# An output projection by seven products of quarters in place of eight, with sums of weight quarters made earlier in the kernel

## The chip, the cores and the metric

The kernel runs on one core of a Trainium2 chip. The metric is the device time of one execution in microseconds (us), the median of 3 runs. Five engines work side by side, each through its own list of instructions in a fixed order: TensorE (PE, matmuls; its weight loads are called PEld), VectorE (DVE), ScalarE (ACT), GpSimd (POOL) and SyncE (SP), which here issues the DMA transfers. A wait holds back all that stands behind it in the same list.

## The reference

One layer on x of 1024 frames by 1024 features, all in float32:

```
h = rmsnorm(x) * norm_w
parts = h @ w_in + b_in             # 5656 columns, cut into 16 segments
y = concat(hgrn2(parts), gla(parts), mlstm(parts))     # 4 heads of 128 from each, 1536 columns
x = x + y @ w_out                   # 1024x1536 by 1536x1024
return rmsnorm(x) * final_norm_w
```

The three mixers are chunked linear attentions with gates: trees of small DVE operations, small matmuls and states. The change touches only the product `y @ w_out`, what feeds it, and the places between the input projections where new work is put.

## The kernel before, in words

**Splitting.** [...] So each operand is kept as a high part (ACT copies and rounds it) and a low part (DVE subtracts the high part from the original), and each product is three matmuls into one PSUM tile: high by high, high by low, low by high. `load_w` (L214 to L228) does it for a weight block of 128x1024: one DMA of 512 KB into `wraw` (two buffers in turn, L222), ACT makes `whi` (L223), DVE makes `wlo` (L224); `whi` and `wlo` have three buffers each. The normalised input lies in sixteen tiles `hT`, `HI[k]` and `LO[k]`.

**Projections.** `projections` (a generator) walks the segments: for the HGRN2 heads h = 0 to 3 the projections f, q, v, z, then q, k, v, z of GLA, then those of the mLSTM, the last one called mz3. `proj_nt` loads a block and runs 24 matmuls of 512 columns for each half, and DVE moves each half out of PSUM (L350). `Weave` puts the small matmuls of the mixers between them by costs written in the generators, and the order of PE is kept as it is written (`manual_schedule`). The order on DVE, ACT and SP is set by the scheduler, and is fixed when the kernel runs. The finished heads go out to DRAM (`ydram`), and the last two, in `ys`, stay on the chip.

**Output projection (L973 to L1073), outside the manual order.** Twelve blocks of `wout` (128x1024) are split, nine of them into the slots of `hT` and others as they come free (L991 to L997). `load_y` brings 128 frames of y back and splits them (L1007 to L1012). There are 8 frame tiles, 2 halves of the columns and 12 blocks k; `out_matmuls` (L1020 to L1022) has the three matmuls of each, so 8 x 2 x 12 x 3 = 576 matmuls of 512 columns. The very last half is done in two parts of 256 columns, so that the page counts 540 of 512 and 72 of 256. `out_part` adds x (L1027), sums squares (ACT, L1029) and multiplies by the norm's weight (L1031); `out_store` finishes the norm and writes (L1036 to L1043).

Of the kernel before, what the change touches and what calls it, by code (L numbers as in the profile page):

```python
# [7 lines left out]
F32 = mybir.dt.float32  # L8
# [6 lines left out]
T = 1024  # L15
# [116 lines left out]
def kernel(ctx: ExitStack, tc: tile.TileContext, x, xt, wt, wide, cols, vbias, wa2, wout, fw, masks, sel,  # L132
# [58 lines left out]
    bq = const.tile([128, 2], F32, name="bq")  # L191

# [38 lines left out]
    HI = [ht.tile([128, T], F32R, name="hT") for _ in range(KC)]  # L231
    LO = [ht.tile([128, T], F32R, name="hT") for _ in range(KC)]
# [168 lines left out]
    def proj_z(name):  # L401
        z, piece = z_piece(name)
        yield from proj_nt(*piece)
        return z
# [400 lines left out]
    def ml_chain(w, r, ready, PQK, Vs, ogs, gates, ys, zs, done):  # L805
# [83 lines left out]
    outs, als, gated, last = [], [], [], []  # L889
    LAST = []  # L890
# [16 lines left out]
    def projections():  # L907
# [54 lines left out]
        LAST.extend(ys)  # L962
# [5 lines left out]

    with tc.manual_schedule(engines={mybir.EngineType.PE}):
        w.run(projections())  # L970
    ys = LAST


    fwb = fp.tile([128, D], F32, name="al", bufs=2)
    nc.sync.dma_start(fwb, bass.AP(tensor=fw.tensor, offset=fw.offset, ap=[[0, 128], [1, D]]))
    WO, raws = [], []
    for k in range(12):
        if k < 3:
            WO.append(load_w(wout[k * 128:(k + 1) * 128, :]))
            continue  # L980
        if k in (3, 5):
            raws = big.tile([128, 2, 1024], F32, name="big")
            raws = [raws[:, 0], raws[:, 1]]
        elif k in (7, 8):
            raws = [wp.tile([128, 1024], F32, name="wraw", bufs=2)]
        elif k == 9:
            raws = [att[:, j].rearrange("p c t -> p (c t)") for j in range(2)]
        elif k == 11:
            raws = [wk.tile([128, 1024], F32, name="S", bufs=1)]
        raw = raws.pop(0)  # L990
        nc.sync.dma_start(raw, wout[k * 128:(k + 1) * 128, :])  # L991
        if k < 11:
            hi, lo = ht.tile([128, 1024], F32R, name="hT"), ht.tile([128, 1024], F32R, name="hT")
        else:
            hi, lo = fp.tile([128, 1024], F32R, name="al", bufs=2), fp.tile([128, 1024], F32R, name="f")
        nc.scalar.activation(hi, raw, AF.Copy)
        nc.vector.tensor_sub(lo, raw, hi.bitcast(F32))  # L997
        WO.append((hi, lo))
    def load_y(i):
        ts = slice(i * 128, (i + 1) * 128)  # L1000
        yh = big.tile([128, 12, 128], F32R, name="big")
        yl = big.tile([128, 12, 128], F32R, name="big")
        yb = big.tile([128, 2, 640], F32, name="big") if i < 2 else None
        for a in (0, 5):
            yr = yb[:, a // 5] if i < 2 else wp.tile([128, 1024], F32, name="wraw", bufs=2)[:, 0:640]
            yr = yr.rearrange("p (k t) -> p k t", k=5)
            nc.sync.dma_start(yr, ydram[a:a + 5, :, ts].rearrange("k p t -> p k t"))  # L1007
            nc.scalar.activation(yh[:, a:a + 5], yr, AF.Copy)
            nc.vector.tensor_sub(yl[:, a:a + 5], yr, yh[:, a:a + 5].bitcast(F32))
        for h in range(2):  # L1010
            nc.scalar.activation(yh[:, 10 + h], ys[h][:, ts], AF.Copy)
            nc.vector.tensor_sub(yl[:, 10 + h], ys[h][:, ts], yh[:, 10 + h].bitcast(F32))  # L1012
        xr = wk.tile([128, D], F32, name="zg")
        nc.sync.dma_start(xr, x[ts, :])
        st = wk.tile([128, 8], F32, name="st", bufs=4)
        return yh, yl, xr, st, (wk.tile([128, 512], F32, name="kd"), wk.tile([128, 512], F32, name="osb"))

    def out_matmuls(p, y, ns, k):
        hi, lo = WO[k]
        nc.tensor.matmul(p, y[0][:, k], hi[:, ns], start=k == 0, stop=False)  # L1020
        nc.tensor.matmul(p, y[0][:, k], lo[:, ns], start=False, stop=False)  # L1021
        nc.tensor.matmul(p, y[1][:, k], hi[:, ns], start=False, stop=k == 11)  # L1022

    def out_part(p, y, ns, part):

        xr, st, xo = y[2:]
        nc.vector.tensor_add(xr[:, ns], p, xr[:, ns])  # L1027
        sq = wk.tile([128, 768], F32, name="qm")
        nc.scalar.activation(sq[:, 0:ns.stop - ns.start], xr[:, ns], AF.Square, accum_out=st[:, part:part + 1])  # L1029
        h = ns.start // 512  # L1030
        nc.vector.tensor_mul(xo[h][:, ns.start - 512 * h:ns.stop - 512 * h], xr[:, ns], fwb[:, ns])  # L1031

    def out_store(i, y, parts):
        st, xo = y[3:]
        if parts == 3:
            nc.gpsimd.tensor_add(st[:, 0:1], st[:, 0:1], st[:, 1:2])  # L1036
        nc.vector.tensor_scalar(st[:, 4:5], st[:, 0:1], 1.0 / D, EPS, op0=OP.mult, op1=OP.add)
        nc.vector.scalar_tensor_tensor(st[:, 5:6], st[:, parts - 1:parts], 1.0 / D, st[:, 4:5], op0=OP.mult, op1=OP.add)
        nc.gpsimd.tensor_tensor(st[:, 6:7], st[:, 5:6], mhalf[:, 0:1], op=OP.pow)
        nc.scalar.activation(xo[0], xo[0], AF.Copy, scale=st[:, 6:7])  # L1040
        nc.vector.tensor_scalar(xo[1], xo[1], st[:, 6:7], None, op0=OP.mult)
        for h in (1, 0):
            nc.sync.dma_start(out[i * 128:(i + 1) * 128, 512 * h:512 * h + 512], xo[h])  # L1043

    halves = [slice(0, 512), slice(512, D)]
    tiles = [load_y(0), load_y(1)]
    ps = [[pl.tile([128, 512], F32, name=nm) for _ in range(2)] for pl, nm in ((pmain, "pm"), (po, "po"))]
    for k in range(12):
        for y, pp in zip(tiles, ps):
            for half in range(2):  # L1050
                out_matmuls(pp[half], y, halves[half], k)
    for i in range(NC):
        y = tiles[i] if i < 2 else load_y(i)
        parts = halves if i < NC - 1 else [halves[0], slice(512, 768), slice(768, D)]
        for a, ns in enumerate(parts):
            if i < 2:
                p = ps[i][a]
            else:
                p = pmain.tile([128, 512], F32, name="pm")[:, 0:ns.stop - ns.start]
                for k in range(12):  # L1060
                    out_matmuls(p, y, ns, k)
            out_part(p, y, ns, a)
        out_store(i, y, len(parts))


def _layout(inputs):
# [78 lines left out]
```

## Time and profile before

| | us |
|---|---|
| median of 3 runs (lowest, highest) | 777.31 (776.87, 777.75) |
| profiled execution: its own time | 775.69 |
| its span in the trace | 773.9 |
| PE busy in the span | 764.1 (99%) |
| DVE, ACT, POOL busy | 411.8, 331.6, 67.1 |
| start of the first matmul of the output projection | 634.01 |
| start of the last matmul | 767.14 |

The span is the time from the first to the last instruction in the trace; 1.8 us of the profiled execution lie outside it. The profiled execution is 1.6 us below the median. Matmuls overlap, so that the time one costs is the distance from its start to the next start, not its length.

### The profile page before, as it was taken

What the parts mean: (1) busy time and instruction counts of PE and PEld (TensorE: products, weight loads), DVE (VectorE), ACT (ScalarE), POOL (GpSimd) and SP (SyncE); (2) the same over time, 40 slices, a digit from 0 to 9 for tenths busy, and PEclk for the clock granted to TensorE, in tenths of its full rate; (3) what the DMA queues carried; (4) which work ended last, traced back from release to release, by engine and by line L of the source; (5) the groups of instructions that cost most, each with busy time, mean ns of one, the idle gap of its engine ahead of it and who ended that gap; (6) DMA issues with size and microseconds to landing.
All of it is one profiled execution on the core that took longest, in us unless ns stands there. A gap on an engine that the chain in (4) does not pass through costs nothing.

```text
span 773.9 us, 14500 instructions
## 1 busy us (share of the span) xinstructions
PE 764.1 (99%) x5991; PEld 660.9 (85%) x5991; DVE 411.8 (53%) x923; ACT 331.6 (43%) x747; POOL 67.1 (9%) x107
## 2 busy tenths in 40 slices
PE   9999999999999999999999999999999999999996
PEld 6889887898887898889988899988899988888886
DVE  7886577584467257325732755343754473532332
ACT  7553689532625404271324532552614592332211
POOL 2001210010200100040001300110000000100000
PEclk9999999999999999999999999999999999999999
DMA  8410120012021102112010202032204342252211
GB/s 284 133 55 26 58 87 28 30 56 62 28 83 33 52 30 63 55 39 72 23 68 28 82 28 63 9 83 87 74 8 165 108 151 89 94 172 90 89 54 55
DMA packets 29810, 55.96 MB, mean 72 GB/s; under 512 B 2656, under 2 KB 16480, under 8 KB 29744
## 3 DMA queue, kind: packets, MB, share of 16 engines
q1 hardware_dynamic: 29072, 54.51, 21.6%
q8 instruction: 47, 0.77, 0.4%
q0 software_dynamic: 672, 0.53, 0.3%
q14 instruction: 19, 0.16, 0.1%
HBM read 45.39 MB, written 9.63 MB: 71 GB/s over the span
## 4 chain that ended last, share of the span: by engine, by line
PE 89%; ACT 4%; DVE 2%; issue 2%; DMA 1%; SPq 1%; POOL 0%; POOLq 0%; DVEq 0%; ACTq 0%
PE pm L338 11%; PE pm L340 11%; PE pm L339 11%; PE pm L370 9%; PE pm L371 8%; PE pm L372 8%; PE pm L1022 5%; PE pm L1020 5%; PE pm L1021 5%; PE po L573 2%; PE po L575 2%; PE pt L558 1%; PE pt L488 1%; PE tp L532 1%; PE pt L457 1%
## 5 line engine op out<-in xcount | busy, mean ns | idle before, releaser
L338 PE MATMUL pm<-hT,whi 128*128 128x512 f32 x400 | 162.5, 406 | 0.0
L340 PE MATMUL pm<-hT,wlo 128*128 128x512 f32 x400 | 156.3, 391 | 0.0
L339 PE MATMUL pm<-hT,whi 128*128 128x512 f32 x400 | 156.2, 391 | 0.0
L370 PE MATMUL pm<-whi,hT 128*128 128x256 f32 (+1 forms) x488 | 142.7, 292 | 0.0
L371 PE MATMUL pm<-wlo,hT 128*128 128x256 f32 (+1 forms) x488 | 138.4, 284 | 0.0
L372 PE MATMUL pm<-whi,hT 128*128 128x256 f32 (+1 forms) x488 | 138.3, 283 | 0.0
L223 ACT ACTIVATE whi<-wraw 128x1024 fp32r<-128x1024 f32 (+4 forms) x50 | 48.7, 977 | 113.1 <-PE pm L372 57.0
L370 PEld LDWEIGHTS pm<-whi,hT 128*128 128x128 f32 x488 | 93.1, 191 | 3.1 <-issue 2.2
L371 PEld LDWEIGHTS pm<-wlo,hT 128*128 128x128 f32 x488 | 93.3, 191 | 0.3
L372 PEld LDWEIGHTS pm<-whi,hT 128*128 128x128 f32 x488 | 93.2, 191 | 0.0
L340 PEld LDWEIGHTS pm<-hT,wlo 128*128 128x128 f32 x400 | 75.1, 188 | 16.6
L338 PEld LDWEIGHTS pm<-hT,whi 128*128 128x128 f32 x400 | 75.2, 188 | 16.0 <-issue 1.5
L339 PEld LDWEIGHTS pm<-hT,whi 128*128 128x128 f32 x400 | 75.3, 188 | 13.5
L224 DVE TENSOR_TENSOR wlo<-wraw,whi 128x1024 fp32r<-128x1024 f32 (+4 forms) x50 | 55.9, 1122 | 18.5 <-ACT whi L223 18.5
L377 DVE SCALAR_TENSOR_TENSOR big<-pm,rs,vb 128x256 f32<-128x256 f32 x72 | 32.0, 454 | 51.0 <-PE pm L372 50.7
L1020 PE MATMUL pm<-hT,big 128*128 128x512 f32 (+1 forms) x120 | 45.4, 378 | 0.0
L1022 PE MATMUL pm<-hT,big 128*128 128x512 f32 (+1 forms) x120 | 45.4, 378 | 0.0
L1021 PE MATMUL pm<-hT,big 128*128 128x512 f32 (+1 forms) x120 | 45.2, 376 | 0.0
L499 ACT ACTIVATE att<-dc 32x128 f32<-32x128 f32 (+1 forms) x48 | 16.5, 344 | 48.6 <-DVE dc L479 48.1
L1027 DVE TENSOR_TENSOR zg<-pm,zg 128x512 f32<-128x512 f32 (+1 forms) x15 | 9.8, 653 | 50.6 <-PE pm L1022 33.8
L350 DVE TENSOR_TENSOR f<-pm,RSB 128x512 f32<-128x512 f32 x18 | 12.4, 687 | 39.0 <-PE pm L340 38.9
L350 DVE TENSOR_TENSOR zg<-pm,RSB 128x512 f32<-128x512 f32 x22 | 15.2, 690 | 31.0 <-PE pm L340 30.9
(303 smaller groups left out, 1317.4 us busy)
## 6 DMA issues: line engine op xcount, KB each, us to landing
wraw<-in_wt_dram SPq DMA_DIRECT2D x39, 512.0 KB, 3.5
zg<-in_x_dram SPq DMA_DIRECT2D x8, 512.0 KB, 3.9
wraw<-ydram SPq DMA_DIRECT2D x12, 320.0 KB, 3.6
big<-in_xt_dram SPq DMA_DIRECT2D x5, 512.0 KB, 4.9
wraw<-in_wout_dram SPq DMA_DIRECT2D x5, 512.0 KB, 4.3
ydram<-zg SPq DMA_DIRECT2D x8, 256.5 KB, 2.1
big<-in_wout_dram SPq DMA_DIRECT2D x4, 512.0 KB, 6.9
out_dram<-kd SPq DMA_DIRECT2D x8, 256.0 KB, 2.4
```

The lines of the kernel that those rows point to most:

```text
L223: nc.scalar.activation(hi[:, s], raw[:, s], AF.Copy)
L224: nc.vector.tensor_sub(lo[:, s], raw[:, s], hi[:, s].bitcast(F32))
L338: nc.tensor.matmul(p, hi[:, ks], HI[k][:, s], start=k == 0, stop=False)
L339: nc.tensor.matmul(p, hi[:, ks], LO[k][:, s], start=False, stop=False)
L340: nc.tensor.matmul(p, lo[:, ks], HI[k][:, s], start=False, stop=k == KC - 1)
L370: nc.tensor.matmul(p, HI[k][:, ts], hi[:, ks], start=k == 0, stop=False)
L371: nc.tensor.matmul(p, HI[k][:, ts], lo[:, ks], start=False, stop=False)
L372: nc.tensor.matmul(p, LO[k][:, ts], hi[:, ks], start=False, stop=k == KC - 1)
L377: nc.vector.scalar_tensor_tensor(dst, p, rs[:, c:c + 1], b, op0=OP.mult, op1=OP.add)
L1020: nc.tensor.matmul(p, y[0][:, k], hi[:, ns], start=k == 0, stop=False)
L1021: nc.tensor.matmul(p, y[0][:, k], lo[:, ns], start=False, stop=False)
L1022: nc.tensor.matmul(p, y[1][:, k], hi[:, ns], start=False, stop=k == 11)
```

## The change

The output projection is cut into quarters: frames in two halves, the 1536 columns of y in two halves of 768, the columns of the result in two halves of 512. A11, A12, A21, A22 are the quarters of y (first figure frames), and `wq[0]` to `wq[3]` those of the weights, which the host now lays out as [4, 3, 128, 1024]. Seven products of quarters, in the order 1, 2, 6, 7, 5, 4, 3, take the place of eight. Each has 4 tiles of 128 frames, 6 blocks of 128 in the depth, and 3 matmuls of 512 columns; the last tile of the last product is again done in two parts of 256. Forms of y (sums and differences of quarters) are made in place by DVE: `s2` (L1050 to L1052, 18 subtractions of 128x512) and `s1` (L1057, 6). `a_form` splits a form (ACT L1040, DVE L1041, six each of 128x512), `b_form` loads and splits three blocks of weights (L1027 to L1029). Products that share an output are added in PSUM where they follow each other (1 and 2, 6 and 7), otherwise by DVE.

Four of the weight forms are sums of quarters. `sum_steps` makes them in 12 steps between the projections: each loads two blocks of 512 KB into the two `wraw` buffers, adds them (DVE, L979), and writes 512 KB to `wsum` in DRAM. The order of PE in the output projection is now fixed as written. PE's order before it is the same as it was.

```
+    wsum = tc.dram_tile([4, 3, 128, 1024], F32, name="wsum")
+    def sum_steps():
+        for dst, a, b in ((0, wq[0], wq[1]), (2, wq[1], wq[3]), (1, wsum[0], wq[3]), (3, wsum[1], wq[2])):
+            for i in range(3):
+                ra, rb = (wp.tile([128, 1024], F32, name="wraw", bufs=2) for _ in range(2))
+                nc.sync.dma_start(ra, a[i])
+                nc.sync.dma_start(rb, b[i])
+                nc.vector.tensor_add(ra, ra, rb)
+                nc.sync.dma_start(wsum[dst, i], ra)
+                yield
+    sums = sum_steps()
...
                 for pce in pieces:
                     yield from proj_nt(*pce)
+                    next(sums, None)
...
                 zs.append((yield from proj_z(f"z{h}")))
+                next(sums, None)
...
             Q, K = yield from gla_qk(r)
+            next(sums, None)
...
                 zs.append((yield from proj_z(f"gz{2 * r + a}")))
+                next(sums, None)
...
-    HI = [ht.tile([128, T], F32R, name="hT") for _ in range(KC)]
-    LO = [ht.tile([128, T], F32R, name="hT") for _ in range(KC)]
+    HI, LO = zip(*[[ht.tile([128, T], F32R, name="hT") for _ in range(2)] for _ in range(KC)])
...
+                dst = y_tile(4 + h)[:, 1] if r else ys[h]
+                nc.vector.tensor_mul(dst[:, s], ys[h][:, s], zs[h][:, 1 + 512 * half:513 + 512 * half])
...
+        hts = [ht.tile([128, 1024], F32R, name="hT") for _ in range(16)]
+        w0 = [wp.tile([128, 1024], F32R, name=nm, bufs=3) for _ in range(3) for nm in ("whi", "wlo")]
+        ASET = [hts[0:6], hts[6:12]]
+        BSET = [w0, hts[12:16] + al2]
...
+        def s2(i):
+            t = wk.tile([128, 768], F32, name="qm")[:, 0:512]
+            nc.vector.tensor_sub(A11(i), A21(i), A11(i))
+            nc.vector.tensor_sub(t, A22(i), A11(i))
+            nc.vector.tensor_sub(A12(i), A12(i), t)
+            return t
...
+        def product(c, p, a, b, first, last, cols=slice(0, 512)):
+            for i in range(6):
...
+                nc.tensor.matmul(p[:, cols], ahi, bhi, start=first and i == 0, stop=False, skip_group_check=True)
+                nc.tensor.matmul(p[:, cols], ahi, blo, start=False, stop=False, skip_group_check=True)
+                nc.tensor.matmul(p[:, cols], alo, bhi, start=False, stop=last and i == 5, skip_group_check=True)
...
+        a1, b1 = a_form(A11), b_form(wq[0])
...
+        for c in range(4):
+            product(c, pa[c], a1, b1, True, False)
+            nc.scalar.activation(P1[:, c], pa[c], AF.Copy)
+        a2, b2 = a_form(A12), b_form(wq[2])
+        for c in range(4):
+            product(c, pa[c], a2, b2, False, True)
+        a6, b6 = a_form(s2), b_form(wsum[1])
...
```

In SP's list, from one load of projection weights early in the kernel on, these are the transfers of the kernel before (`wt` are weights of a projection, `vb` is a bias):

```order
L222 DMA wraw<-in_wt_dram 128x1024 x3
L357 DMA vb<-in_vbias_dram 128x256
L222 DMA wraw<-in_wt_dram 128x1024 x3
L517 DMA ydram<-zg 128x511
L514 DMA ydram<-zg 128x513
```

and these those of the changed one from the same load on, with the numbers of the buffers (`wq` are quarters of the output weights):

```order
L224 DMA wraw_904<-in_wt_dram 128x1024
L977 DMA wraw_1108<-in_wq_dram 128x1024
L978 DMA wraw_1109<-in_wq_dram 128x1024
L980 DMA wsum_479<-wraw_1108 128x1024
L224 DMA wraw_1114<-in_wt_dram 128x1024
L977 DMA wraw_1193<-in_wq_dram 128x1024
L358 DMA vb_1735<-in_vbias_dram 128x256
L978 DMA wraw_1194<-in_wq_dram 128x1024
L980 DMA wsum_479<-wraw_1193 128x1024
L224 DMA wraw_1200<-in_wt_dram 128x1024
```

Between any two of these weights now stand two loads and a write, and of the two buffers in turn the first holds L977's block until it is written, the second takes L978's block and then the next weight.

On DVE, where the tree of head 1 begins, before (L350 is the last half of q, L433 and L438 the tree, L695 and L696 a GLA gate):

```order
L437 TENSOR_TENSOR f<-f 128x128
L350 TENSOR_TENSOR zg<-pm,RSB 128x512
L695 TENSOR_SCALAR po<-po,pc 128x512 x2
L696 TENSOR_TENSOR al<-po,al 128x512
L433 COPY_PREDICATED dc<-mk_88,pt 128x32x3
L438 TENSOR_TENSOR big<-big,f 128x128x3
```

and after (each line number one higher):

```order
L351 TENSOR_TENSOR zg<-pm,RSB 128x512
L979 TENSOR_TENSOR wraw<-wraw 128x1024
L696 TENSOR_SCALAR po<-po,pc 128x512 x2
L434 COPY_PREDICATED dc<-mk_88,pt 128x32x3
L439 TENSOR_TENSOR big<-big,f 128x128x3
```

The sum of one step (L979, the fifth of the twelve) now stands ahead of the tree.

On DVE at the passage to the output projection the kernel before has this (the two L350 are the first and the last half of mz3, L997 the low parts of `wout` blocks, L1009 and L1012 those of y):

```order
L350 TENSOR_TENSOR zg<-pm,RSB 128x512
L997 TENSOR_TENSOR hT<-big,hT 128x1024
L833 TENSOR_TENSOR f<-f,zg 128x512
L997 TENSOR_TENSOR hT<-big,hT 128x1024
L1012 TENSOR_TENSOR big<-f,big 128x128
L997 TENSOR_TENSOR hT<-big,hT 128x1024
L350 TENSOR_TENSOR zg<-pm,RSB 128x512
L997 TENSOR_TENSOR hT<-big,hT 128x1024
L1009 TENSOR_TENSOR big<-big 128x640 x2
```

The changed one has, behind the first half of mz3, two L1041, an L1050, an L835 and an L1050, and then this (L1041 are low parts of A11 and then of A12, the L351 is the last half of mz3, and the L1029 is the low part of the third weight block of product 1):

```order
L1051 TENSOR_TENSOR qm<-big 128x512
L1057 TENSOR_TENSOR big<-big 128x512
L1041 TENSOR_TENSOR hT<-big,hT 128x512 x2
L1051 TENSOR_TENSOR qm<-big 128x512
L1057 TENSOR_TENSOR big<-big 128x512
L1041 TENSOR_TENSOR hT<-big,hT 128x512
L1041 TENSOR_TENSOR hT<-att,hT 128x512
L1041 TENSOR_TENSOR hT<-big,hT 128x512
L351 TENSOR_TENSOR zg<-pm,RSB 128x512
L1041 TENSOR_TENSOR hT<-big,hT 128x512
L1050 TENSOR_TENSOR big<-big 128x512 x2
L1029 TENSOR_TENSOR wlo<-wraw,whi 128x1024
```

From the first L1041 to the L1029 that is 18 operations of 128x512: eight L1041, eight of `s1` and `s2`, one L835 and one L351.

## Rows read from the trace of the kernel before

**Rows 1.** Which engines are busy, over the whole span (page).

```profile
PE 764.1 (99%) x5991; PEld 660.9 (85%) x5991; DVE 411.8 (53%) x923; ACT 331.6 (43%) x747; POOL 67.1 (9%) x107
```

**Rows 2.** By stretch: us, busy us by engine, PE's granted clock, DMA share, GB/s.

```profile
614.80:624.00 9.20, 9.20 (x48) 7.70 (x47) 4.47 (x12) 7.73 (x25) 2.42 (x4) 1.00 0.76 242
...
634.00:767.50 133.50, 133.42 (x613) 109.66 (x611) 48.12 (x92) 34.22 (x74) 6.34 (x9) 1.00 0.28 89
```

**Rows 3.** The same for L1020 alone, one of the three matmul lines.

```profile
634.00:768.00 134.00, 77.30 (x204) 38.16 (x203) 1.00 0.27 89
```

**Rows 4.** PE in order of time: start, length, then what ran; the output projection's first matmul.

```profile
634.01 0.39 PE L1020 MATMUL pm<-whi,big 128*128 128x512 f32 x1
```

**Rows 5.** PE in order of time, matmuls of 256 columns.

```profile
760.38 0.28 PE L1020 MATMUL pm<-hT,big 128*128 128x256 f32 x1
760.49 0.28 PE L1021 MATMUL pm<-hT,big 128*128 128x256 f32 x1
```

**Rows 6.** In order of time, the end: last matmul, last store's issue.

```profile
767.14 0.28 PE L1022 MATMUL pm<-al,big 128*128 128x256 f32 x1
770.27 0.38 SPq L1043 DMA_DIRECT2D out_dram<-kd  x1
```

**Rows 7.** In order of time, DVE and PE around the passage.

```profile
627.76 0.69 DVE L833 TENSOR_TENSOR f<-f,zg 128x512 f32<-128x512 f32 x1
628.37 0.68 DVE L350 TENSOR_TENSOR zg<-pm,RSB 128x512 f32<-128x512 f32 x1
629.67 0.40 PE L340 MATMUL pm<-hT,wlo 128*128 128x512 f32 x1
634.44 0.68 DVE L350 TENSOR_TENSOR zg<-pm,RSB 128x512 f32<-128x512 f32 x1
```

**Rows 8.** Groups of DVE from 600 us: busy us, mean ns, idle before.

```profile
L1031 DVE TENSOR_TENSOR kd<-zg,al 128x512 f32<-128x512 f32 x8 | 5.5, 689 | 0.9 <-DMA out_dram<-kd 0.7
```

**Rows 9.** In order of time, splitting of weights: ACT, DVE, SP's next load.

```profile
47.24 1.23 DVE L224 TENSOR_TENSOR wlo<-wraw,whi 128x1024 fp32r<-128x1024 f32 x1 [0.42 <-ACT whi L223]
48.49 0.33 SPq L222 DMA_DIRECT2D wraw<-in_wt_dram  x1
73.31 2.39 DVE L224 TENSOR_TENSOR wlo<-wraw,whi 128x1024 fp32r<-128x1024 f32 x2
92.30 1.06 ACT L223 ACTIVATE whi<-wraw 128x1024 fp32r<-128x1024 f32 x1
104.28 1.06 ACT L223 ACTIVATE whi<-wraw 128x1024 fp32r<-128x1024 f32 x1 [2.80 <-PE pm L339]
```

**Rows 10.** DMA issues (page): KB each, median us to landing.

```profile
wraw<-in_wt_dram SPq DMA_DIRECT2D x39, 512.0 KB, 3.5
ydram<-zg SPq DMA_DIRECT2D x8, 256.5 KB, 2.1
```

**Rows 11.** In order of time, tree of head 1: DVE's first and PE's wait.

```profile
110.46 0.69 DVE L350 TENSOR_TENSOR zg<-pm,RSB 128x512 f32<-128x512 f32 x1 [1.65 <-PE pm L340]
111.39 1.42 DVE L695 TENSOR_SCALAR po<-po,pc 128x512 f32<-128x512 f32 x2 [0.23 <-PE po L682]
122.75 0.45 PE L457 MATMUL pt<-big 128*32 128x16 f32 x32 [0.39 <-DVE dc L433]
```

**Rows 12.** By stretch, as 2, behind the last matmul.

```profile
767.50:771.50 4.00, 0.00 (x0) 0.00 (x0) 1.45 (x4) 1.23 (x3) 0.54 (x1) 1.00 0.20 77
771.50:772.00 0.50, 0.00 (x0) 0.00 (x0) 0.00 (x0) 0.00 (x0) 0.00 (x0) 0.68 1.01 389
```

**Rows 13.** PE in order of time, the kernel's first matmuls.

```profile
7.70 0.63 PE L296 MATMUL pm<-hT,whi 128*128 128x512 f32 x1
8.12 0.63 PE L297 MATMUL pm<-hT,whi 128*128 128x512 f32 x1
10.61 0.40 PE L297 MATMUL po<-hT,whi 128*128 128x512 f32 x1
10.84 0.39 PE L298 MATMUL po<-hT,wlo 128*128 128x512 f32 x1
```

More of the change, by code (lines that the diff above doesn't have):

```diff
@@ L131, with kernel @@
 @with_exitstack
-def kernel(ctx: ExitStack, tc: tile.TileContext, x, xt, wt, wide, cols, vbias, wa2, wout, fw, masks, sel,
+def kernel(ctx: ExitStack, tc: tile.TileContext, x, xt, wt, wide, cols, vbias, wa2, wq, fw, masks, sel,
                       ident_in, out):
@@ L191 @@
     bq = const.tile([128, 2], F32, name="bq")
+    fwb = const.tile([128, D], F32, name="fwb")
+    P1 = const.tile([128, 4, 512], F32, name="P1")
     def lower_bound():
@@ L967, in gla_tail, with y_tile @@
                         lambda: len(outs) >= 8 + 4 * r and len(vs) > 0, outs)
+    Y = {}
+    def y_tile(i):
+        if i not in Y:
+            Y[i] = att.rearrange("p h c t -> p h (c t)") if i == 5 else \
+                big.tile([128, 2, 1040], F32, name="big")[:, :, 0:T]
+        return Y[i]
     with tc.manual_schedule(engines={mybir.EngineType.PE}):
         w.run(projections())
[L971 to L975 removed]
@@ L976 @@
[L976 to L1031, printed above, removed]
@@ L1045 @@
[L1045 to L1063, printed above, removed]
+        nc.sync.dma_start(fwb, bass.AP(tensor=fw.tensor, offset=fw.offset, ap=[[0, 128], [1, D]]))
@@ new lines @@
+        for i in (0, 1, 2, 3):
+            y_tile(i)
+        for kh in range(2):
+            for i in range(6):
+                if kh * 6 + i < 10:
+                    for th in range(2):
+                        s = slice(512 * th, 512 * th + 512)
+                        nc.sync.dma_start(Y[i][:, kh, s], ydram[6 * kh + i, :, s])
+        hts = [ht.tile([128, 1024], F32R, name="hT") for _ in range(16)]
+        w0 = [wp.tile([128, 1024], F32R, name=nm, bufs=3) for _ in range(3) for nm in ("whi", "wlo")]
@@ new lines, with b_form @@
+        al2 = [fp.tile([128, 1024], F32R, name="al", bufs=2) for _ in range(2)]
+        ASET = [hts[0:6], hts[6:12]]
+        BSET = [w0, hts[12:16] + al2]
+        made = [0, 0]
+        def b_form(src):
+            t = BSET[made[1] % 2]
+            made[1] += 1
+            for i in range(3):
+                raw = wp.tile([128, 1024], F32, name="wraw", bufs=2)
+                nc.sync.dma_start(raw, src[i])
+                nc.scalar.activation(t[2 * i], raw, AF.Copy)
+                nc.vector.tensor_sub(t[2 * i + 1], raw, t[2 * i].bitcast(F32))
+            return t
@@ new lines, in a_form @@
+        def a_form(src):
+            t = ASET[made[0] % 2]
+            made[0] += 1
+            for i in range(6):
+                s = slice(512 * (i % 2), 512 * (i % 2) + 512)
+                raw = src(i)
+                hi, lo = t[i // 2 * 2][:, s], t[i // 2 * 2 + 1][:, s]
+                nc.scalar.activation(hi, raw, AF.Copy)
+                nc.vector.tensor_sub(lo, raw, hi.bitcast(F32))
+            return t
+        quarter = lambda th, kh: lambda i: Y[i][:, kh, 512 * th:512 * th + 512]
@@ new lines, with load_x @@
+        stats = const.tile([128, NC, 8], F32, name="stats")
+        U2 = [wk.tile([128, 512], F32, name=nm) for nm in ("osb", "osb", "kd", "kd")]
+        xt_of = [fp.tile([128, T], F32, name="f") for _ in range(3)] + [wk.tile([128, 1 + T], F32, name="zg")[:, 0:T] for _ in range(2)] \
+            + [wk.tile([128, 1024], F32, name="S", bufs=1), RSB]
+        xt_of = [[t[:, 0:512], t[:, 512:1024]] for t in xt_of]
+        junk = dc.rearrange("p h c x -> p (h c x)")
+        def load_x(cs):
+            for c in cs:
+                if c == 7:
+                    xt_of.append([wk.tile([128, 768], F32, name="qm")[:, 0:512] for _ in range(2)])
+                for h in range(2):
+                    nc.sync.dma_start(xt_of[c][h], x[128 * c:128 * c + 128, 512 * h:512 * h + 512])
@@ new lines, in xs, with rows_done, store @@
+        def xs(c, cols):
+            h = cols.start // 512
+            return xt_of[c][h][:, cols.start - 512 * h:cols.stop - 512 * h]
+        def rows_done(c, cols, part):
+            xr = xs(c, cols)
+            nc.scalar.activation(junk[:, 0:cols.stop - cols.start], xr, AF.Square, accum_out=stats[:, c, part:part + 1])
+            nc.vector.tensor_mul(xr, xr, fwb[:, cols])
+        def store(c, parts):
+            st, xr = stats[:, c], xt_of[c]
+            if parts == 3:
+                nc.gpsimd.tensor_add(st[:, 0:1], st[:, 0:1], st[:, 1:2])
+            nc.vector.tensor_scalar(st[:, 4:5], st[:, 0:1], 1.0 / D, EPS, op0=OP.mult, op1=OP.add)
+            nc.vector.scalar_tensor_tensor(st[:, 5:6], st[:, parts - 1:parts], 1.0 / D, st[:, 4:5], op0=OP.mult, op1=OP.add)
+            nc.gpsimd.tensor_tensor(st[:, 6:7], st[:, 5:6], mhalf[:, 0:1], op=OP.pow)
+            nc.scalar.activation(xr[0], xr[0], AF.Copy, scale=st[:, 6:7])
+            nc.vector.tensor_scalar(xr[1], xr[1], st[:, 6:7], None, op0=OP.mult)
+            for h in (1, 0):
+                nc.sync.dma_start(out[c * 128:(c + 1) * 128, 512 * h:512 * h + 512], xr[h])
@@ new lines @@
+        L, R = slice(0, 512), slice(512, D)
+        banks = lambda tags: [pl.tile([128, 512], F32, name=nm) for pl, nm in tags for _ in range(2)]
+        tags_a, tags_b = ((pmain, "pm"), (po, "po")), ((ptree, "pt"), (ptr, "tp"))
+        a1, b1 = a_form(A11), b_form(wq[0])
+        pa = banks(tags_a)
+        load_x(range(4))
+        for c in range(4):
+            product(c, pa[c], a1, b1, True, False)
+            nc.scalar.activation(P1[:, c], pa[c], AF.Copy)
+        a2, b2 = a_form(A12), b_form(wq[2])
@@ new lines @@
+        for c in range(4):
+            product(c, pa[c], a2, b2, False, True)
+        a6, b6 = a_form(s2), b_form(wsum[1])
+        pb = banks(tags_b)
+        for c in range(4):
+            nc.vector.tensor_add(xs(c, L), pa[c], xs(c, L))
+            rows_done(c, L, 0)
+        for c in range(4):
+            product(c, pb[c], a6, b6, True, False)
+            nc.vector.tensor_sub(U2[c], P1[:, c], pb[c])
+        a7, b7 = a_form(A11), b_form(wsum[2])
+        load_x(range(4, NC))
+        for c in range(4):
+            product(c, pb[c], a7, b7, False, True)
+            nc.vector.tensor_sub(P1[:, c], P1[:, c], pb[c])
+            nc.vector.tensor_sub(xs(c, R), xs(c, R), U2[c])
@@ new lines @@
+        a5, b5 = a_form(s1), b_form(wsum[0])
+        pa = banks(tags_a)
+        for c in range(4):
+            product(c, pa[c], a5, b5, True, False)
+            nc.vector.tensor_sub(xs(c + 4, R), xs(c + 4, R), P1[:, c])
+            nc.vector.tensor_add(xs(c + 4, R), pa[c], xs(c + 4, R))
+            rows_done(c + 4, R, 1)
+        a4, b4 = a_form(A22), b_form(wsum[3])
+        pb = banks(tags_b)
+        for c in range(4):
+            product(c, pb[c], a4, b4, True, True)
+            nc.vector.tensor_add(xs(c + 4, L), P1[:, c], xs(c + 4, L))
+            nc.vector.tensor_add(xs(c + 4, L), pb[c], xs(c + 4, L))
+            rows_done(c + 4, L, 0)
+            store(c + 4, 2)
@@ L1066, in _layout @@
+        a3, b3 = a_form(A12), b_form(wq[3])
+        for c in range(4):
+            parts = [R] if c < 3 else [slice(512, 768), slice(768, D)]
+            for n, cols in enumerate(parts):
+                pc_ = slice(cols.start - 512, cols.stop - 512)
+                product(c, pa[c], a3, b3, False, True, pc_)
+                nc.vector.tensor_add(xs(c, cols), pa[c][:, pc_], xs(c, cols))
+                rows_done(c, cols, 1 + n)
+            store(c, 1 + len(parts))
 def _layout(inputs):
```

30 lines of the change are left out of this document (13 added, 17 removed).

## The prediction

> **What bounds the kernel now.** I read the busy times first: PE works for 764.1 of 773.9 us, every other engine for half of that or less [rows 1]. Then the stretch that the change rewrites: from the first matmul of the output projection to the last PE has no gap worth naming (133.42 us busy in 133.5), while DVE works 48.12 us and the DMA engines 0.28 of the time [rows 2]. So time falls away only where matmuls do, and any wait that is put on PE is paid in full, unless it falls behind the last matmul. The row for one of the three matmul lines counts 204 [rows 3], so 612 in all: 540 of 512 columns and 72 of 256. The first starts at 634.01 [rows 4], the last at 767.14 and, with 0.28 us, ends at 767.42 [rows 6]: 133.4 us. Matmuls of 256 columns start 0.11 us apart [rows 5]. That leaves (133.4 - 72 x 0.11) / 540 = 0.232 us for one of 512. Behind the last matmul come 6.5 us of norm and store, which the change keeps in form: the last piece is again of 256 columns, and the store is again two transfers (the second is issued at 770.27 before [rows 6]).
>
> **Term 1, matmuls removed.** 7 x 4 x 6 x 3 = 504 in place of 576. By form it is 486 of 512 columns and 36 of 256: 486 x 0.2324 + 36 x 0.11 = 116.9 us. That is 16.5 less. The other bound is an eighth of the whole, 133.4 / 8 = 16.7. Nothing hides beside it, because PE was busy throughout.
>
> **Term 2, the passage to product 1.** Before, PE goes on from the last projection without a gap (busy before and after 634 [rows 2]), since three blocks of `wout` had been split in advance. Product 1 needs three blocks too, but `whi` and `wlo` have three buffers, and one of them holds the weights of mz3 until its last matmul. So the third block can be split only behind 634.2. What decides is DVE's list, which is fixed. Its subtraction for that third block (L1029) stands behind 18 operations of 128x512 that begin with the first low part of A11. That first one needs HI[0], whose last reader starts at 629.67 and takes 0.40 us [rows 7]; ACT's copy needs 0.6 us more, so DVE begins at about 630.8. Operations of 512 columns follow each other at 0.61 us when DVE has work queued (627.76 to 628.37 [rows 7]); alone one takes 0.689 [rows 8]. 18 of them last 11.0 to 12.4 us, then the subtraction itself 1.23 [rows 9]: the low part is there at 643.0 to 644.4. One among the 18 is the eviction of mz3's last half, which could run at 634.44 before [rows 7], earlier than its turn comes here, so it adds no wait. PE, which starts product 1 at 634.01, wants this block at its 14th matmul (first tile, fifth block of depth): 634.0 + 13 x 0.232 = 637.0. PE waits 6.0 to 7.4 us. I take +6.5. Lower bound 3, if DVE can start on the forms earlier than I read; upper bound 9, if the loads of y come late, since two `s1` operations ahead of that subtraction read the last pieces: 20 transfers of 256 KB are 5.2 MB, and at 242 GB/s [rows 2] that takes 21 us. If they start where that stretch does, at 614.8, and come in the order in which they are issued, the two thirds that those 18 operations read are there at 629, all at 636; I take no delay.
>
> **Term 3, the clock.** [...] What half speed costs is seen at the kernel's beginning: matmuls start 0.42 us apart (7.70, 8.12) until about 10.5, then 0.23 (10.61, 10.84) [rows 13]; some ten matmuls of the slow kind cost 10 x 0.2 = 2.0 us. Bounds 0 and +2.5; I take +1.5, nearer to the row.
>
> [...]
>
> **Term 4, the sums between the projections.** 12 steps: 24 loads of 512 KB, 12 additions of 128x1024, 12 writes of 512 KB. The additions cost DVE 12 x 1.2 = 15 us, by the subtraction of the same size [rows 9]. DVE has room in the mean, but its order is fixed, and so is that of SP. The two `wraw` buffers now work as one ring: L977's block sits in one until it is summed and written, and the other takes in turn L978's block and the next weight. One period is: load 3.5 [rows 10], addition 1.2, SP's issue 0.33 (it comes 0.02 us behind the end of the subtraction that frees the buffer: 47.24 + 1.23 = 48.47, and 48.49 [rows 9]), load of the weight 3.5 [rows 10], ACT 1.06, DVE's low part 1.23 [rows 9], and about 0.6 for handing over and for issue: 11.4 us. The weights of the kernel before are split 12.0 us apart at the densest place that matters (92.30 and 104.28 [rows 9]), so the ring just keeps up, and weights come about two projections ahead of their use: no weight is late for PE. But an addition that stands in DVE's list ahead of its data holds the operations behind it.
> Walk from the low part of head 1's first weights, which ends (the pair, 73.31 + 2.39) at 74.5 for the first of the two: load and addition end at 79.3; three periods on, the fifth addition ends at 79.3 + 3 x 11.4 = 113.5, or at 115.4 with 12.0 a period. It stands right behind the eviction that ends at 111.2 and ahead of the gate and the tree of head 1, which started at 111.39 [rows 11]. DVE runs through from there, and PE already waits 0.39 us for it at 122.75 [rows 11]: no slack at all. So that wait grows by 2 to 4 us; I take 3.5. The other eleven additions each put 1.2 us into DVE's list, and stand at places with weights further apart than at this densest one, so the data are there: I take +1.0 for all of them, bounds 0 and 4. The writes of 512 KB have no row; 256 KB land in 2.1 us [rows 10], twice as much should need 2.1 to 4.2, and the block's buffer has a whole period, so nothing. Together +4.5, bounds +1 and +9.
>
> **Term 5, the rest of the output projection.** A product lasts 72 x 0.232 = 16.7 us on PE. In it DVE must split a form: 6 x 0.69 + 3 x 1.23 = 7.8 us, and evict 4 tiles with 1 to 4 operations of 0.69 each. Over the stage I count 119 operations of 512 columns and 19 of 1024, 95 to 105 us of DVE in about 123: twice as much as before and near to full, but still under PE. Walking the list, the tightest passage is product 6, whose `s2` brings 18 more operations: its last low part ends at 668 to 671, PE wants it at about 674. The passages to 7, 5, 4 and 3 have 4 us or more. I take 0, bounds 0 and +6.
>
> **Sum.** -16.5 + 6.5 + 1.5 + 4.5 + 0 = -4.0 on the profiled execution: 775.69 - 4.0 = 771.7. The median lies 1.62 above that execution (777.31), so **773.3**.
>
> **Rivals.**
> A. The waits are not there: DVE gets to the third block in time, and the additions find their data. Then -16.5 + 0 to 2, so 761 to 763. For it: DVE idles half of the span [rows 1]. Against it: the order of both passages is fixed, and at 110 us DVE had no gap.
> B. Slower than before: the ring. If SP, whose list has the write of the sum ahead of the load of the weight, holds that load back until the write has landed (2.1 to 4.2 us, 2.8 taken), a period is 11.4 + 2.8 = 14.2. Then each weight of head 1, wanted every 12 us [rows 9], comes later than the last: the fifth addition ends at 79.3 + 3 x 14.2 = 121.9, 8.4 later than above, and the tree of head 1 with it. Heads 2 and 3 have the same sequence; further apart, I put 2 us on each. That is 4.5 + 8.4 + 4 = 17 in place of 4.5: 785.8. It decides from a period of about 13 us on. For it: the 3.5 us of a load are a median [rows 10]. Against it: the write does not share the buffer that the weight goes into.
> C. DVE becomes the bound in the output projection, with waits of 1 to 2 us at each of six passages: +6 to +10, so 779 to 783. For it: its 95 to 105 us in 123. Against it: the walk.
> D. No gain of matmul time, because products that interleave with waits run at the low clock for longer: 72 more matmuls at 0.42 give +14, so 787. It needs PE to wait again and again, which only C would bring.
>
> **How the numbers follow.** Forecast (the sum within its bounds, 767 to 778) 0.58; A 0.17; B 0.13; C 0.09; D 0.03. The measurement of this kernel can tell about 0.2%, 1.55 us, from no change: faster is below 775.8, slower above 778.9. Of the forecast's own 0.58 I put 0.47 below 775.8, 0.09 within and 0.02 above; A is faster; B, C and D are slower but for 0.03 of C that is the same. Faster 0.64, same 0.12, slower 0.24. The range that leaves out 0.1 on either side goes from 763, in the middle of A's end, to 782, in C and the near side of B.
>
> **What would show it.** 504 matmuls in some 117 us of busy PE; a wait of 6 to 7 us on PE at the 14th matmul of product 1, ended by DVE's L1029 (`wlo`), with a granted clock of half behind it; a wait of about 4 us at the tree of head 1 in place of 0.39, ended by DVE, with L979 waiting for a load just before it; no wait at the first matmul of products 2 to 3. It would be wrong if the first wait is missing (A), if waits at trees of heads 2 and 3 are as long (B), or if PE waits for L1041 or L1029 at later products (C).

## The result and the profile after

The changed kernel takes 769.60 us in the median (768.51 to 771.40, four executions), beside 777.09 for the kernel before: a ratio of 0.9908, 95% interval 0.9881 to 0.9934, or 7.5 us less. The forecast was 773.3 in a range of 763 to 782, and faster. The profiled execution took 770.62 (span 768.8), 5.1 us less than the profiled one of before; two of the four, at a mean clock of 0.994 where this one has 0.990, took 2.1 us less again.

The page after, engines and DMA, beside [rows 1] and [rows 10]; the last two lines are new:

```profile
PE 750.4 (98%) x5901; PEld 648.4 (84%) x5901; DVE 471.6 (61%) x998; ACT 351.3 (46%) x770; POOL 77.1 (10%) x107
...
wraw<-in_wt_dram SPq DMA_DIRECT2D x39, 512.0 KB, 3.8
wraw<-in_wq_dram SPq DMA_DIRECT2D x27, 512.0 KB, 3.6
...
wsum<-wraw SPq DMA_DIRECT2D x12, 512.0 KB, 2.9
```

PE is still the bound, but it now waits longer: before, its longest wait behind the first two microseconds was 0.6 us. What it waited for in the whole execution, longest first (engine, line, what ended the wait: us, times, longest):

```profile
PE pm L1067 <- DVE wlo L1029: 4.4, 1, 4.4
PE pt L429 <- ACT al L699: 2.0, 1, 2.0
PE tp L847 <- DVE al L844: 1.5, 1, 1.5
PE pt L429 <- DVE f L437: 1.0, 3, 0.4
...
PE po L1066 <- DVE zg L1158: 0.6, 1, 0.6
```

The first is the passage to product 1, the second and one of the three of the fourth lie at the tree of head 1, the other two at 58 and 59 us, the last is at the end. The third is at the kernel's beginning, and was there before.

**The passage.** PE in order of time, beside [rows 4]; product 1 starts here at 638.49, 4.5 us later than the output projection did before:

```profile
638.26 0.39 PE L341 MATMUL pm<-hT,wlo 128*128 128x512 f32 x1
638.49 0.39 PE L1066 MATMUL pm<-whi,hT 128*128 128x512 f32 x1
...
641.21 0.39 PE L1066 MATMUL pm<-whi,hT 128*128 128x512 f32 x1
645.99 0.80 PE L1067 MATMUL pm<-wlo,hT 128*128 128x512 f32 x1 [4.39 <-DVE wlo L1029]
646.58 0.63 PE L1068 MATMUL pm<-whi,hT 128*128 128x512 f32 x1
647.01 0.63 PE L1066 MATMUL pm<-whi,hT 128*128 128x512 f32 x1
...
651.28 0.58 PE L1067 MATMUL pm<-wlo,hT 128*128 128x512 f32 x1
651.70 0.40 PE L1068 MATMUL pm<-whi,hT 128*128 128x512 f32 x1
```

The 14th matmul waits, for the low part named in the forecast, and from it on matmuls start 0.43 us apart instead of 0.227, until 651.7: half clock, 13 steps in 5.71 us where 2.95 would do, 2.8 us. The granted clock of that stretch (behind the busy times, as in [rows 2]) is 0.50; in the standstill itself, 641.60 to 645.99, it is 0.87 in the mean (1.00 up to 644.60, 0.50 from 645.00 on):

```profile
645.99:651.70 5.71, 5.71 (x14) 4.47 (x14) 5.71 (x9) 1.65 (x2) 5.71 (x1) 0.50 0.28 95
```

DVE in the same stretch, beside [rows 7]:

```profile
633.87 1.30 DVE L1041 TENSOR_TENSOR hT<-big,hT 128x512 fp32r<-128x512 f32 x2 [0.35 <-PE tp L533]
635.08 0.69 DVE L1050 TENSOR_TENSOR big<-big 128x512 f32<-128x512 f32 x1
...
643.51 1.29 DVE L1050 TENSOR_TENSOR big<-big 128x512 f32<-128x512 f32 x2
644.71 1.22 DVE L1029 TENSOR_TENSOR wlo<-wraw,whi 128x1024 fp32r<-128x1024 f32 x1
```

No idle time stands between: 18 operations in 10.84 us, then the one that PE waits for, done at 645.93.

**The tree of head 1.** DVE, beside [rows 11], ACT, PE's wait, and the stretch behind it:

```profile
111.88 0.68 DVE L351 TENSOR_TENSOR zg<-pm,RSB 128x512 f32<-128x512 f32 x1
114.69 1.23 DVE L979 TENSOR_TENSOR wraw<-wraw 128x1024 f32<-128x1024 f32 x1 [2.13 <-DMA wraw<-in_wq_dram]
115.83 1.41 DVE L696 TENSOR_SCALAR po<-po,pc 128x512 f32<-128x512 f32 x2
...
119.77 1.28 ACT L699 ACT_TABLE_LOAD   x1 [0.85 <-DVE al L697]
122.20 0.55 PE L429 MATMUL pt<-qm,big 128*32 128x48 f32 x32 [1.96 <-ACT al L699]
...
123.00:126.40 3.40, 3.27 (x39) 2.72 (x40) 3.40 (x11) 3.35 (x6) 0.07 (x1) 0.55 0.26 64
```

The fifth addition waits 2.13 us for its load and runs 1.2; the gate that started at 111.39 before starts at 115.83. Its last step on ACT (L699), which had to wait for DVE's L697, is what ends PE's wait. Behind the wait the granted clock fell here too: 0.55 in this stretch, and five matmuls of 512 columns take 2.22 us from 123.92 on where 1.15 would do, 1.1 us more.

### The profile page after: what moved, and what is told of

It is laid out like the page before. It is cut to its first block, busy times and chain, and to the rows that moved or that the text cites. A ratio compares the mean times of both kernels' runs of the same rounds, so it can differ in the third digit from the quotient of the medians.

```text
span 768.8 us, 14522 instructions
## 1 busy us (share of the span) xinstructions
PE 750.4 (98%) x5901; PEld 648.4 (84%) x5901; DVE 471.6 (61%) x998; ACT 351.3 (46%) x770; POOL 77.1 (10%) x107
## 4 chain that ended last, share of the span: by engine, by line
PE 81%; DMA 7%; DVE 6%; ACT 3%; issue 2%; SPq 0%; POOL 0%; POOLq 0%; DVEq 0%; ACTq 0%
PE pm L339 10%; PE pm L341 9%; PE pm L340 9%; PE pm L371 8%; PE pm L372 7%; PE pm L373 7%; DMA wraw<-in_wq_dram 2%; DMA wraw<-in_wt_dram 2%; PE po L574 2%; DMA big<-ydram 2%; PE pm L1067 1%; PE pm L1068 1%; PE pm L1066 1%; PE pt L489 1%; PE po L576 1%
## 5 line engine op out<-in xcount | busy, mean ns | idle before, releaser
L225 ACT ACTIVATE whi<-wraw 128x1024 fp32r<-128x1024 f32 (+4 forms) x47 | 45.6, 973 | 106.3 <-PE pm L373 55.8
L226 DVE TENSOR_TENSOR wlo<-wraw,whi 128x1024 fp32r<-128x1024 f32 (+4 forms) x47 | 52.4, 1117 | 27.6 <-ACT whi L225 27.5
L399 POOL COPY zg<-zg 128x1 f32<-128x1 f32 x12 | 18.6, 1548 | 220.1 <-ACT zg L397 220.1
L500 ACT ACTIVATE att<-dc 32x128 f32<-32x128 f32 (+1 forms) x48 | 16.5, 344 | 49.4 <-DVE dc L480 48.9
L211 POOL TENSOR_SCALAR st<-st 128x4 f32<-128x4 f32 x24 | 4.9, 206 | 267.4 <-ACT sq L525 267.4
L351 DVE TENSOR_TENSOR f<-pm,RSB 128x512 f32<-128x512 f32 x18 | 12.4, 688 | 30.8 <-PE pm L341 30.7
L525 ACT ACTIVATE sq<-po 128x128 f32<-128x128 f32 x64 | 17.8, 278 | 27.9 <-PE po L581 23.4
L397 ACT ACTIVATE zg<-zg,pc 128x512 f32<-128x512 f32 x24 | 17.2, 719 | 29.0 <-DVE zg L351 28.9
L351 DVE TENSOR_TENSOR zg<-pm,RSB 128x512 f32<-128x512 f32 x22 | 15.2, 691 | 24.7 <-PE pm L341 24.5
```

The costliest lines, as they stand in the source:

```text
L225: nc.scalar.activation(hi[:, s], raw[:, s], AF.Copy)
L226: nc.vector.tensor_sub(lo[:, s], raw[:, s], hi[:, s].bitcast(F32))
L351: nc.vector.tensor_mul(dst(half), p, RSB[:, s])
L399: nc.gpsimd.tensor_copy(z[:, 0:1], z[:, T:T + 1])
L525: nc.scalar.activation(sq, o[:, j, :], AF.Square, accum_out=st[:, j:j + 1])
```

## The experiments

Each is an edit of the changed kernel. e1 to e4 were timed beside the kernel before on one chip (777.05 there), e5 to e8 on another (777.16). Ratios are to the kernel before, with 95% intervals. The changed kernel was not timed again beside them: differences from its 769.60 are taken across these series, and its own four executions spread from 768.51 to 771.40.

**e1, without the sums.**

```
-    sums = sum_steps()
+    sums = iter(())
...
-        a6, b6 = a_form(s2), b_form(wsum[1])
+        a6, b6 = a_form(s2), b_form(wq[1])
```

(the other three likewise)

> Leaves out the twelve sums: the four products that use them load quarters of the weights as they are, so the result is not the reference's; everything else stays. Theory (the sums cost only at the tree of head 1, where an addition that waits for its load stands ahead of the tree): mz3's last matmul comes at about 633.8 as in the kernel before (638.26 with the sums), the wait at that tree is back to about 0.4 us, and the time falls by 4 to 5 us against the changed kernel, to 764 to 766. Rival (the additions and transfers cost everywhere a little, or nothing): the shift of PE stays above 2 us, the time falls by less than 2.

Measured: 765.44, ratio 0.9842 (0.9826 to 0.9859). PE's wait at the tree is the old one, and mz3 ends early:

```profile
121.88 0.45 PE L458 MATMUL pt<-big 128*32 128x16 f32 x32 [0.41 <-DVE dc L434]
...
632.85 0.39 PE L341 MATMUL pm<-hT,wlo 128*128 128x512 f32 x1
633.07 0.39 PE L1066 MATMUL pm<-whi,hT 128*128 128x512 f32 x1
```

The sums cost 4.2 us in the medians. Product 1 starts 5.4 us earlier than with them, and 0.9 earlier than the output projection did before; PE is that much ahead already at 40 us, so this part is not of the sums. Product 1's wait stays at 4.4 us: the two losses do not depend on each other.

**e2, the two sums of head 1's projections later.**

```
                     yield from proj_nt(*pce)
-                    next(sums, None)
+                    if h > 1:
+                        next(sums, None)
```

> The two steps of sums between the projections of head 1 move to later places; all twelve are still made. Theory (place, not amount: only at head 1 does the tree on DVE have no slack): PE's shift before the output projection falls from 4.5 to under 1.5 us, time lower by 3 to 4.5 against the changed kernel, 765 to 767. Rival (the ring of two buffers is too slow for any head): the same wait of about 4 us at the tree of head 2 or 3, time within 1 us of the changed kernel.

Measured: 766.94, ratio 0.9864 (0.9849 to 0.9879), 2.7 us less than the changed kernel where 3 to 4.5 were expected, and a shift of 1.5 us (PE's delay at product 1 against the first matmul of the old output projection, 634.01). The theory holds in its main part, and behind the wait at the tree matmuls start 0.23 us apart again from 121.18 on; a rest remains, since one addition still lies ahead of the tree:

```profile
111.91 1.23 DVE L980 TENSOR_TENSOR wraw<-wraw 128x1024 f32<-128x1024 f32 x1 [1.48 <-DMA wraw<-in_wq_dram]
113.06 0.69 DVE L351 TENSOR_TENSOR zg<-pm,RSB 128x512 f32<-128x512 f32 x1
...
120.02 0.89 PE L429 MATMUL pt<-qm,big 128*32 128x48 f32 x64 [1.91 <-DVE f L437]
```

**e3, the third block of product 1 into other buffers.**

```
-        BSET = [w0, hts[12:16] + al2]
+        BSET = [w0[0:4] + al2, hts[12:16] + w0[4:6]]
```

> The third weight block of product 1 is split into two buffers that are free early, and the buffer that mz3 holds goes to product 2. Theory (the 4.4 us wait is that block's place in DVE's list behind 18 operations): the wait at the 14th matmul goes, and with it the half clock behind it (2.6 us), so 4.4 to 7 us less than the changed kernel, 762.5 to 765; the next late thing is a low part of A11 at under 1.5 us. Rival (DVE, 100 of 126 us busy in this stage, is the bound): the wait comes back at product 2 or 6, and the time falls by less than 2.

Measured: 770.71, ratio 0.9914 (0.9899 to 0.9929), no gain: the rival's result. The first wait is gone as the theory says, but another came in product 6, with matmuls 0.43 us apart behind it (682.03, 682.46, 682.88). Waits of PE in the output projection:

```profile
PE pt L1068 <- DVE hT L1041: 3.7, 1, 3.7
PE po L1066 <- DVE zg L1158: 0.6, 1, 0.6
PE pm L1066 <- DVE zg L351: 0.3, 1, 0.3
```

The rival's reason is not what the trace shows, though. DVE did not run out of time; it stood idle for 6.7 us before product 6, and the chain of what it waited for goes back over ACT, a load and SP to GpSimd:

```profile
645.34 16.75 POOL L399 COPY zg<-zg 128x1 f32<-128x1 f32 x1 [12.69 <-ACT zg L397]
...
662.11 0.80 SPq L1082 DMA_DIRECT2D zg<-in_x_dram  x2
663.02 12.10 SPq L1027 DMA_DIRECT2D wraw<-wsum  x4
...
668.85 1.06 ACT L1028 ACTIVATE whi<-wraw 128x1024 fp32r<-128x1024 f32 x1 [9.02 <-DMA wraw<-wsum]
...
669.95 1.23 DVE L1029 TENSOR_TENSOR wlo<-wraw,whi 128x1024 fp32r<-128x1024 f32 x1 [6.70 <-ACT whi L1028]
```

GpSimd's copy of one column of mz3's z took 16.75 us; the load of x into that tile waited for it at the head of SP's list, and behind that load stood the weights of product 6. In the changed kernel the same copy took 13.40 us, but there PE was late itself by its first wait and found everything ready. The first wait had covered the second.

**e4, matmuls in place of the standstill.**

```
+                if first and i == 4 and c == 0 and warm:
+                    z = warm.pop()
+                    for _ in range(18):
+                        nc.tensor.matmul(z, a[0][:, 0:128], b[0][:, 0:512], start=True, stop=True, ...)
```

> 18 extra matmuls of 512 columns, whose result nobody reads, are put on PE where it waits in product 1. Theory (the clock fell because PE stood still): they fit into the wait (18 x 0.227 = 4.1 of 4.4 us), no matmul behind it runs at half speed, the last matmul comes 2.6 us earlier than in the profile of the changed kernel, about 759.4, and the executions lie close together, 767.5 to 769. Rival (the clock falls for another reason, or the extra matmuls push the rest): matmuls 0.43 us apart stay, or the time rises by up to 4.

Measured: 768.38 (768.17 to 769.60), ratio 0.9888 (0.9873 to 0.9902). The wait shrinks to 0.32 us, and the matmuls behind it start 0.23 us apart from the second on:

```profile
646.88 0.39 PE L1070 MATMUL pm<-whi,hT 128*128 128x512 f32 x1
647.59 0.50 PE L1071 MATMUL pm<-wlo,hT 128*128 128x512 f32 x1 [0.32 <-DVE wlo L1029]
647.92 0.39 PE L1072 MATMUL pm<-whi,hT 128*128 128x512 f32 x1
648.15 0.40 PE L1070 MATMUL pm<-whi,hT 128*128 128x512 f32 x1
```

The output projection lasts 120.9 us from its first matmul to its last instead of 123.5, so the standstill's half clock cost 2.6 us there. The last matmul came at 761.0 and not at 759.4, because this execution reached product 1 at 640.1, 1.6 us later, by waits at the beginning and at the tree of head 1, which the edit does not touch. In the medians the gain is 1.2, not 2.6, and less than the spread of the changed kernel, two of whose four executions were at 768.5 anyway.

**e5, e3 without GpSimd's copy for the mLSTM's z** (its column is read only for the other heads).

```
-            if half:
+            if half and not name.startswith("mz"):
                 nc.gpsimd.tensor_copy(z[:, 0:1], z[:, T:T + 1])
```

> As e3, and GpSimd's copy of one column, which nothing reads for the mLSTM's z, is left out for these. Theory (in e3 the copy took 16.75 us beside DVE's two-input operations, held SP at a load of x until 662.1, and with that the second weight block of product 6, DVE and PE): that block is loaded before 657, DVE's idle 6.7 us before it goes, the 3.7 us wait of PE in product 6 and its half clock go: 5 us less than e3, 765 to 766.5, the output projection under 118.5 us from its first matmul to its last. Rival (DVE has too much work before product 6 anyway): PE still waits over 2 us there, time within 1.5 us of e3.

Measured: 765.30, ratio 0.9846 (0.9829 to 0.9864). PE in the output projection (us, busy by engine, granted clock, DMA share, GB/s) and its waits:

```profile
639.00:757.00 118.00, 116.89 (x527) 96.13 (x525) 96.25 (x156) 56.32 (x99) 4.01 (x8) 1.00 0.40 130
```

116.9 us from first to last, granted clock 1.00, and no wait but the 0.3 and 0.6 us of e3's last two lines: DVE's 96 us fit beside PE.

**e6, the copy alone left out.** The edit of e5 without that of e3.

> Control: only GpSimd's copy for the mLSTM's z is left out of the changed kernel. Theory (there the 13.4 us copy holds SP for 3.8 us, but the wait of PE is in product 1, before it): no change, 768.5 to 770.5, PE's 4.4 us wait stays. [...]

Measured: 770.40, ratio 0.9909 (0.9894 to 0.9925), the wait of 4.4 us as before. So the copy costs nothing as long as the first wait is there, and the gain of e5 over e3 needs both edits.

**e7, everything.** e5, and the sums placed so:

```
-                for pce in pieces:
+                for n, pce in enumerate(pieces):
                     yield from proj_nt(*pce)
-                    next(sums, None)
+                    if h == 3 or (h == 2 and n == 0):
+                        next(sums, None)
```

> e5, and the sums moved so that none lies between the second weights of head 2 and the tree of head 1; all twelve are made. Theory (the three losses add up): PE's shift before the output projection under 0.5 us (4.5 in the changed kernel), no wait over 1 us in the output projection, no stretch at half clock: 760 to 761.5. Rival (the sums wait elsewhere, at heads 2 or 3): 762.5 to 764.

Measured: 761.37 (761.10 to 762.66), ratio 0.9798 (0.9781 to 0.9815), the fastest version, 8.2 us below the changed kernel. The output projection lasts 116.9 us, and its waits are two:

```profile
PE po L1067 <- DVE zg L1159: 0.6, 1, 0.6
PE pm L1067 <- DVE zg L351: 0.3, 1, 0.3
```

The time is in the expected range, but one part of the theory was not met: PE's shift before the output projection was 3.2 us in the profiled execution, the slowest of the four, where under 0.5 was expected: 1.2 us of it is a wait for a small transfer at 105 us, the rest in waits of 0.4 to 1.2 between 119 and 400. The mean clock of that execution is 0.997, where the changed kernel's profiled one has 0.990. I did not take the waits apart.

**e8, the additions on GpSimd.**

```
-                nc.vector.tensor_add(ra, ra, rb)
+                nc.gpsimd.tensor_add(ra, ra, rb)
```

> The twelve additions run on GpSimd in place of DVE. Theory (the loss at head 1 is that an addition waits in DVE's list): DVE goes on, PE's shift before the output projection falls to under 1.5 us, 765 to 766.5. Rival (GpSimd is held off while DVE runs two-input operations, as its copy was): additions last over 3 us each, the buffers come free later, weights are split later, and the time is the same or up to 6 us more, 769 to 776.

Measured: 775.93, ratio 0.9991 (0.9974 to 1.0007): all the gain gone. Of ten executions eight lie between 774.72 and 777.21, one took 780.79, and one 2587.77, which the ratio leaves out and no trace explains. The theory's forecast fell, and the rival's was right in time, but not by the mechanism that it gave: the additions are not held off.

```profile
79.23 2.38 POOL L979 TENSOR_TENSOR wraw<-wraw 128x1024 f32<-128x1024 f32 x1 [3.90 <-DMA wraw<-in_wq_dram]
93.09 2.39 POOL L979 TENSOR_TENSOR wraw<-wraw 128x1024 f32<-128x1024 f32 x1 [4.19 <-DMA wraw<-in_wq_dram]
107.57 2.39 POOL L979 TENSOR_TENSOR wraw<-wraw 128x1024 f32<-128x1024 f32 x1 [2.40 <-issue]
122.04 2.34 POOL L979 TENSOR_TENSOR wraw<-wraw 128x1024 f32<-128x1024 f32 x1 [11.72 <-DMA wraw<-in_wq_dram]
```

They run 2.4 us each, and follow each other every 14 us where DVE's come every 12. Weights come later with them, and it is now their low part that waits in DVE's list at the tree (116.98, below); and beside one of GpSimd's additions (122.04 to 124.38) the DVE operation that starts at 122.19 takes 2.47 us, its like a few rows earlier 0.45.

```profile
116.98 1.22 DVE L226 TENSOR_TENSOR wlo<-wraw,whi 128x1024 fp32r<-128x1024 f32 x1 [1.61 <-ACT whi L225]
...
121.54 0.45 DVE L421 TENSOR_TENSOR qm<-big,f 128x256 f32<-128x256 f32 x1
...
122.19 2.47 DVE L421 TENSOR_TENSOR qm<-big,f 128x256 f32<-128x256 f32 x1
...
PE pt L429 <- DVE f L437: 4.7, 1, 4.7
```

The last line is PE's wait there, 4.7 us, and PE reaches product 1 about 5 us later than in the changed kernel.

## Why the prediction was right

It was right in sign and by its main mechanisms; the sum was 1.1 us too high on the profiled execution and 3.7 on the median. That it came so near is in part luck: term 2 was too high by 2.1 us and term 3 too low by 1.2.

| term | forecast | profiled execution | shown by |
|---|---|---|---|
| 1, matmuls | -16.5 | -17.4: 133.4 to 116.0 | e5: 116.9, less 0.9 of waits |
| 2, wait in product 1 | +6.5 | +4.4 | e3: gone there |
| 3, half clock behind it | +1.5 | +2.6 to 2.8 | e4: 2.6 |
| 4, sums | +4.5 | +4.5: 634.01 to 638.49 | e1: 4.2 in the medians, 5.4 at product 1 |
| 5, rest of the stage | 0 | +0.6, and +0.3 behind the last matmul | the page |

Term 1 was a little small because a matmul of 512 columns, 0.232 us apart from the next in the old output projection, is 0.227 in most of the new one; why, no run here separates.

Term 2 had the right matmul, the right block and the right 18 operations; its size failed at one row. I let DVE begin at 630.8 because I took the matmul at 629.67 [rows 7] for the last reader of HI[0]. The row after shows DVE's first L1041 released by the transposes (L533) that stand behind the first three matmuls of that half, one block of depth sooner. DVE began 4.6 us ahead of PE's first matmul, not 3.2, and the wait was shorter by that much and by the quick pace of the 18.

Term 3 was put below its row [rows 13] for no good reason, and came out above its upper bound of +2.5: 13 matmuls at half speed, granted clock 0.50, cost 2.6 to 2.8 us. No run shows the term as it was put: that a wait of 6.5 us brings half clock was the author's estimate, and its row shows a pace alone, with a granted clock of 1.00 in the record of that stretch (7.70 to 10.50). What the runs showed in its place: in the wait of 4.4 us the clock is 1.00 for the first 3.0 us and 0.50 in the last, then 0.50 up to 651.70 and 1.00 behind it; and in e4, where PE does useless work instead of standing still and waits 0.32 us, matmuls start 0.23 us apart from the second on.

Term 4 came out to the half microsecond at the place and by the addition that were named: the fifth ended at 115.9, forecast 113.5 to 115.4. (The 0.6 us for handing over in the period of 11.4 was the author's estimate; the additions came 12.0 us apart.) Its size is in part luck. PE was 0.7 us ahead before the first load of a sum (the same transposes, before and after):

```profile
39.79 1.09 PE L268 MATMUL tp<-ident,rs 128*128 128x128 f32 x8 [0.47 <-POOL rs L262]
39.09 1.09 PE L269 MATMUL tp<-ident,rs 128*128 128x128 f32 x8 [0.74 <-POOL rs L263]
```

So from there to product 1 PE lost some 5.2 us, and in e1, without the sums, nothing. Some 3.6 of it lie at the tree of head 1, where the forecast had one wait of 3.5, ended by DVE: the same matmuls start 0.7 us later than before ahead of the tree (117.25 and 117.95) and 4.3 later behind it (137.65 and 141.94). They are waits of 2.0, 0.4 and 0.4 us, the longest ended by ACT behind DVE, and 1.1 us of half clock, which the forecast counts at product 1 alone; before, PE waited 0.4 there. The other 1.6, forecast as 1.0, came for the most part before 100 us. e2 shows that it is the place, and e8 suggests that the period of the ring counts as well: at 14 us rival B's condition (above 13) is met, and its wait at head 1 appears, with a time of 775.9; that it costs less than the 785.8 given there fits PE's shift, which is 7.6 us behind head 1 and 9.7 at product 1: heads 2 and 3 add little. (Some of the 7.6 is DVE's operation of 2.47 us beside GpSimd's addition, so the period alone was not measured.)

Term 5, the walk to product 6, left 3 to 6 us of room. That room was lent by the wait of term 2. e3 took it away, and the walk had missed what then came late: it counted DVE's work and not SP's list, with a load of x that waits for a copy on GpSimd. The rivals are out for the changed kernel: the two passages did wait (A); its additions at head 1 come 12.0 us apart (they start at 90.66, 102.64 and 114.69), and no tree of heads 2 and 3 waits over 0.2 us (B); e5 shows DVE's 96 us beside PE's 117 with less than 1 us of waiting, and e7 has no more (C); the half clock lasts for 13 matmuls and five (D).

The median lies lower than the profiled execution suggests because that was one of the two longer ones. What differs between them no run here took apart; a stretch of half clock less would fit their mean clocks (0.990 and 0.994), but in e6, where the clocks spread as far, the times lie within 0.9 us.

## What to carry to other kernels

A block that one version has ready before a stage begins may find no free buffer in the next version: for every operand of the first product, look where its last operation stands in the list of the engine that makes it, and what frees its buffer. Work squeezed into gaps costs by its place in a fixed list, not by its length: 15 us of additions cost 4 to 5, most of it at one tree without slack, and making two of the twelve later got 2.7 back. A wait costs more than its length where the clock falls behind it (here 4.4 us, and 2.6 to 2.8 more at a granted clock of 0.50), and no list of waits shows that: read the granted clock as well. After taking a wait away, look for the one that it covered, on queues too: e3's edit alone gained nothing, leaving out the copy alone (e6) nothing, both together (e5) over 4 us.

## What I had not expected of the hardware

GpSimd's copy of 128x1 takes 0.19 us at 632.46 in e3, with DVE idle, and 13.40 and 16.75 us at the passage, where DVE runs operations on two SBUF tiles back to back. In the changed kernel it ends at 657.22, as DVE falls idle (657.17); in e3 at 662.09, just after DVE starts an operation with one operand in PSUM (L1123, 661.96). And in e8 a DVE operation beside GpSimd's addition of two tiles takes 2.47 us for 0.45, and ends at 124.66, just behind the addition (124.38). At the passage the copy lasted through a whole run of DVE's operations. But the same copy for the z before it (630.59, changed kernel) took only 0.62 us: it ended at 631.21, right behind DVE's L1029 (631.18), though DVE's next operation on two SBUF tiles (L835) had begun at 631.13. What let it through there and not between the operations at the passage is open.
